# Five depthwise-convolution products of one channel tile on ScalarE and GpSimd, and a new plan

## The chip, the cores and the metric

The kernel runs on one core of a Trainium2 chip. The metric is the device time of one execution in microseconds (us), as the median of several runs. A core has TensorE (PE in the profile; its weight loads are PEld), VectorE (DVE), ScalarE (ACT), GpSimd (POOL) and SyncE (SP), which here only issues transfers. Each engine works through its own instruction list in order, and waits on semaphores for the others.

## What is computed

One layer of a decoder: 1024 prompt tokens and 8 sample tokens share all weights; the width is 1024.

```python
h = rmsnorm(x, g_mix);  u = h @ w_in                  # 1024 -> 512 pool, 512 value, 512 gate
glu = val * sigmoid(gate)                             # 512 channels
ya = pool_mixer(a)                                    # trailing means over 2/4/8/16 tokens, a linear map per group
yb = silu(layernorm(depthwise_conv31(glu) + b_dw))    # causal, 31 taps per channel
x = x + concat(ya, yb) @ w_out
x = x + cross_attn(rmsnorm(x, g_attn), mk, mv, w_q, w_o)   # 4 heads, 256 memory tokens
x = x + (silu(h @ w_gate) * (h @ w_up)) @ w_down      # h = rmsnorm(x, g_ffn)
y = rmsnorm(x, g_final)
```

Samples use cached keys and values and stored histories; the prompt's keys and values come from `mem_prompt` (`m @ w_k`, `m @ w_v`), and are outputs too, as are the new histories.

## The kernel before

Activations lie with channels on the 128 partitions and tokens along the free axis, even prompt tokens first (512), then odd (512), then the 8 samples. Every fp32 matmul is done as three passes over operands split in a high and a low part; the split is one copy (`split`, L466 to L479) that rounds, on ScalarE or GpSimd, and one subtraction, on VectorE or GpSimd. `split_by_dma` (L488 to L495) makes the low part with a negated copy and a transfer issued by GpSimd that adds the source.

The program is a list of tasks. Each task names the engines that may do it with a cost, the buffers that it reads and writes and a priority: its number in the list plus an entry of `NUDGE`. A planner, `Program.order` (L216), then walks through a timeline of its own costs and gives each task an engine and a place in that engine's order. `ORDER` is the list of pieces (letter and index) in which tasks are made, `CHOSEN` pins some tasks to one engine, `LEAD` says how many weight blocks ahead a block's loading and splitting are put, `SLACK` and `MARGINS` shape the planner's choice and its costs. Buffers come from tags with a few slots each: 3 scratch buffers (`scr`), 3 raw weights, 2 split weights, and in PSUM 2 of three banks (`mm`) and 2 of one bank (`ms`).

The stages, with their letters. Input projection: groups `g`, `v` (gate and value, four channel tiles) and `A` (pool channels), each a PE group in an `mm` buffer, which VectorE evicts (glu L829, a L935). Convolution of tile cg: with even and odd tokens apart, the 31 taps become two families. `C` (`conv_sums`, L749 to L769) makes 16 products of the sum of even and odd tokens with sums of neighbouring taps, on ScalarE or GpSimd into one of four slots of `cp`, which GpSimd or VectorE add to the odd half of `y`. `D` (`conv_parts`, L771) makes 31 products on VectorE, which fold into two PSUM accumulators `acc[0]` (16) and `acc[1]` (15), one instruction each, multiply and add (L781 for the first, L783 for the others; `cacc` in the profile). L791 to L802 then merge both with `y`. `s` does the sample tokens, `W` and `M` the pooling, `K` and `V` the memory's keys and values (kps, vps; evicted into the scratch buffers kf and vf and stored from there), `L` the layer norm.

`O` and `B` are the output projection, `q` the queries. Attention: scores `S` (L1126; maximum L1134, exponential L1143, normalising L1151), transposes `T` (L1165 to L1170), products `P` (`pv`, L1184 to L1189), and `a` to `e` for the samples, whose cached keys and values are multiplied on VectorE (spcache_k, spcache_v, L1223). `o`, then the pieces `u`, `x`, `y`, `z`, prepare the feed-forward part, which runs as a seven-product scheme (L1429), and the last stage (L1800 to L1857) ends with the final norm.

Of the kernel before, what the change touches and what calls it, by code (L numbers as in the profile page):

```python
# [1986 lines left out]
```

## Time and profile before

| | us |
|---|---|
| median of 3 runs | 1144.47 |
| lowest, highest | 1144.37, 1146.84 |
| the profiled execution | 1144.27 |
| its span, first to last instruction | 1142.5 |
| TensorE busy in it | 1120.8 |
| VectorE, ScalarE, GpSimd busy | 927.6, 499.7, 287.8 |

All rows that are shown come from the one profiled execution. A busy TensorE means that at least one matmul is under way; matmuls overlap, so it says nothing of their rate. In a table by stretch, the columns after each engine's busy time give its instruction count; the granted clock is the share of TensorE's full clock that it was allowed. A row of waits reads: engine and what it was about to do, then the instruction that ended the wait, the time in total, how often, and the longest. A row of a tile's instructions gives the shortest, the median and the longest duration in ns.

### The profile page before, as it was taken

What the parts mean: (1) busy time and instruction counts of PE and PEld (TensorE: products, weight loads), DVE (VectorE), ACT (ScalarE), POOL (GpSimd) and SP (SyncE); (2) the same over time, 40 slices, a digit from 0 to 9 for tenths busy, and PEclk for the clock granted to TensorE, in tenths of its full rate; (3) what the DMA queues carried; (4) which work ended last, traced back from release to release, by engine and by line L of the source; (5) the groups of instructions that cost most, each with busy time, mean ns of one, the idle gap of its engine ahead of it and who ended that gap; (6) DMA issues with size and microseconds to landing.
All of it is one profiled execution on the core that took longest, in us unless ns stands there. A gap on an engine that the chain in (4) does not pass through costs nothing.

```text
span 1142.5 us, 19533 instructions
## 1 busy us (share of the span) xinstructions
PE 1120.8 (98%) x7736; PEld 1067.4 (93%) x7736; DVE 927.6 (81%) x1514; ACT 499.7 (44%) x706; POOL 287.8 (25%) x327
## 2 busy tenths in 40 slices
PE   9999999999999989999999999999999999999996
PEld 8999988999999979999999999999999999999996
DVE  7999999776257886888888888988888798879744
ACT  7766648353243452445233333333433443332444
POOL 2689772133712201433000000000000123332011
PEclk9999999999999999999999999999999999999999
DMA  8444587433485687322424352254433697657612
GB/s 307 94 93 110 127 233 237 163 114 149 165 249 176 207 325 244 123 82 75 140 84 149 128 190 105 100 176 159 156 124 112 237 374 286 242 169 235 186 59 91
DMA packets 66252, 193.54 MB, mean 169 GB/s; under 512 B 8368, under 2 KB 12144, under 8 KB 64880
## 3 DMA queue, kind: packets, MB, share of 16 engines
q1 hardware_dynamic: 62128, 178.81, 43.8%
q0 software_dynamic: 3600, 13.13, 6.6%
q8 instruction: 61, 1.00, 0.4%
q10 hardware_dynamic: 432, 0.36, 0.1%
q14 instruction: 31, 0.25, 0.1%
HBM read 147.84 MB, written 44.43 MB: 168 GB/s over the span
## 4 chain that ended last, share of the span: by engine, by line
PE 78%; DVE 15%; DMA 4%; issue 1%; ACT 1%; POOL 0%; DVEq 0%; SPq 0%; ACTq 0%; POOLq 0%
PE pr L1429 49%; PE po L582 7%; DVE cacc L783 6%; PE ps L582 5%; PE fd L1800 4%; PE oa L582 4%; PE ob L582 4%; DVE spcache_k L1223 1%; PE vps L1027 1%; DMA spcache_k<-in_cache_k 1%; PE kps L949 1%; PE pv L1184 1%; DVE spcache_v L1223 1%; DVE xss L513 1%; DVE x L1854 1%
## 5 line engine op out<-in xcount | busy, mean ns | idle before, releaser
L1429 PEld LDWEIGHTS pr<-ab,wTb 128*128 128x128 f32 x1056 | 123.4, 190 | 2.3 <-issue 0.5
L1429 PE MATMUL pr<-ab,wTa 128*128 128x260 f32 x1056 | 124.9, 275 | 0.0
L1429 PE MATMUL pr<-ab,wTb 128*128 128x260 f32 x1056 | 124.3, 275 | 0.0
L1429 PEld LDWEIGHTS pr<-ab,wTa 128*128 128x128 f32 x1056 | 123.1, 190 | 1.3
L1429 PE MATMUL pr<-ab,wG 128*128 128x512 f32 x528 | 121.1, 380 | 0.0
L1429 PEld LDWEIGHTS pr<-ab,wG 128*128 128x128 f32 x528 | 96.9, 189 | 12.5 <-issue 0.5
L582 PE MATMUL ps<-xop,w 128*128 128x344 f32 x720 | 105.5, 309 | 0.0
L582 PEld LDWEIGHTS ps<-xop,w 128*128 128x128 f32 x720 | 105.0, 189 | 0.0
L1445 DVE TENSOR_TENSOR su<-pr,su 128x520 f32<-128x520 f32 (+1 forms) x112 | 77.3, 692 | 25.9 <-PE pr L1429 25.4
L1429 PEld LDWEIGHTS pr<-hb,dV 128*128 128x128 f32 x768 | 92.3, 190 | 2.2
L1429 PE MATMUL pr<-hb,dV 128*128 128x260 f32 x768 | 92.7, 275 | 0.0
L582 PE MATMUL ps<-xq,w 128*128 128x344 f32 x576 | 87.0, 310 | 0.0
L582 PE MATMUL po<-oo,w 128*128 128x344 f32 x576 | 84.7, 309 | 0.0
L582 PEld LDWEIGHTS po<-oo,w 128*128 128x128 f32 x576 | 84.3, 189 | 0.2
L582 PEld LDWEIGHTS ps<-xq,w 128*128 128x128 f32 x576 | 84.2, 189 | 0.1
L783 DVE SCALAR_TENSOR_TENSOR cacc<-glu,vec,cacc 128x502 f32<-128x502 f32 (+14 forms) x116 | 77.5, 739 | 0.1
L1429 PE MATMUL pr<-hb,dW 128*128 128x512 f32 x288 | 69.2, 379 | 0.0
L1456 POOL MEMSET su<- 128x16 f32 x22 | 2.4, 112 | 255.7 <-PE pr L1429 200.1
L1800 PE MATMUL fd<-ho,w 128*128 128x260 f32 (+1 forms) x432 | 64.3, 311 | 0.0
L1800 PEld LDWEIGHTS fd<-ho,w 128*128 128x128 f32 x432 | 59.8, 190 | 4.4 <-issue 0.5
L1445 DVE TENSOR_TENSOR x<-pr,x 128x512 f32<-128x512 f32 (+1 forms) x76 | 52.3, 690 | 12.7 <-PE pr L1429 11.6
L766 POOL TENSOR_TENSOR y<-y,cp 128x511 f32<-128x511 f32 (+14 forms) x46 | 57.6, 1254 | 14.9 <-DVE y L766 7.2
(314 smaller groups left out, 2164.7 us busy)
## 6 DMA issues: line engine op xcount, KB each, us to landing
gr<-in_w_gu SPq DMA_DIRECT2D x44, 512.0 KB, 3.4
hb<-su SPq DMA_DIRECT2D x16, 520.0 KB, 3.8
hb<-hb SPq DMA_DIRECT2D x16, 520.0 KB, 6.7
dr<-in_w_dn SPq DMA_DIRECT2D x16, 512.0 KB, 4.0
hb<-bh SPq DMA_DIRECT2D x14, 520.0 KB, 3.3
hb<-hb SPq DMA_DIRECT2D x14, 512.0 KB, 7.4
spcache_k<-in_cache_k SPq DMA_DIRECT2D x12, 512.0 KB, 5.2
ho<-hd SPq DMA_DIRECT2D x10, 520.0 KB, 6.3
```

The costliest lines, as they stand in the source:

```text
L513: add({"Pool": pool_tt(n), "DVE": dve(n)}, lambda e: e.tensor_tensor(total(), total(), sq[:, i, :n], ALU.add), [(sq, i), tkey], [tkey], lo ...
L582: e.matmul(placed(ps[:, c, :CW]), w[:, wi, cols], turns(x[:, xi, c * CW : (c + 1) * CW]), start=first and p == 0, stop=last and p == 2)
L766: add({"Pool": pool_tt(HALF), "DVE": dve(HALF)}, lambda e: e.tensor_tensor(yb[:, i, HALF + n : SEQ], yb[:, i, HALF + n : SEQ], cp[:, q, : ...
L783: e.scalar_tensor_tensor(acc[h][:, n:], src[:, : HALF - n], w, acc[h][:, n:], ALU.mult, ALU.add)
L949: e.matmul(placed(ps[:, 0, i * NMEM : (i + 1) * NMEM]), w[:, wi, block_cols(k)], turns(memg[k // 4][:, xi, k % 4]), start=(k == 0 and p == ...
L1027: e.matmul(placed(ps[:, m]), memg[k // 4][:, xi, k % 4, m * P : (m + 1) * P], turns(w[:, wi, col : col + 512]), start=(k == 0 and p == 0), ...
L1184: e.matmul(placed(ps[:, c]), v[:, vi, m, col : col + P], turns(pT[h][m][:, pi, sl]), start=(m == 0 and p == 0), stop=(m == 1 and p == 2))
L1223: e.scalar_tensor_tensor(piece[:, b], piece[:, b], 1.0, bc[:, b], ALU.mult, ALU.mult, accum_out=out(m)[:, first + b : first + b + 1])
L1429: e.matmul(placed(bank(c)), w[:, wi, cols(j)], turns(xs[0](j, xi)[:, c * n : (c + 1) * n]), start=onto is None and j == 0 and p == 0, stop ...
L1445: from_sums(sums, "DVE", dve, lambda e, src, sl: e.tensor_tensor(as_banks(o(sl), src), src, as_banks(a(sl), src), op), [akey], [okey])
L1800: e.matmul(placed(view(i)), w[:, wi, col : col + P], turns(hops[k][:, xi, half, lo - half * HALF + i * width // count : lo - half * HALF + ...
L1854: add({"DVE": dve(n * width)}, lambda e, i=i, n=n: e.tensor_tensor(x2[j][:, i : i + n, sl], x2[j][:, i : i + n, sl], fin[:, sl].unsqueeze( ...
```

## The change

- `conv_parts` for tile 3 (`OFFLOAD = (0, 0, 0, 5)`): the products n = 10 to 14 of the odd family no longer fold into `acc[1]` on VectorE. The first is written by ScalarE into a scratch buffer `part`; each of the other four is written by ScalarE or GpSimd into one of two halves of a second scratch buffer `ahead`, and added to `part` by GpSimd or VectorE. After the 26 products that stay, one addition on VectorE brings `part` into `acc[1]`.
- Normalising the probabilities may be done on ScalarE as well.
- `pv` may use single banks (`PV_MS`, empty), and for product 4 (`PV_FIRST`) both halves' matmuls are listed ahead of the copies.
- A new `ORDER`, `NUDGE` (about three times as many entries), `CHOSEN`, and new numbers in `LEAD`, `DOWN_BY_DMA`, `SLACK` and `MARGINS`.

```diff
 ORDER = (
-    "n0 g1 C0 v1 g2 s0 m6 v2 m1 g3 s1 m3 A1 A3 v3 m7 m4 m5 D0 A0 A2 m0 m2 K0 W3 C1 s3 K1 s2 K2 V1 W0 W1 C2 W2 M0 D1 Y0 M3 V0 "
+    "n0 g1 C0 v1 g2 s0 m5 v2 m1 g3 m7 m6 A1 A3 s1 v3 m3 m4 m0 D0 A0 A2 m2 K0 W3 C1 s3 K1 s2 K2 V1 W0 W1 D1 M3 C2 W2 M0 Y0 V0 "
...
-LEAD = {"w_k": 4, "w_v": 7, "w_out_a": 16, "w_q": 42, "w_in": 22, "w_out_b": 11, "w_o": 14}
+LEAD = {"w_k": 4, "w_v": 7, "w_out_a": 11, "w_q": 36, "w_in": 17, "w_out_b": 11, "w_o": 16}
...
-DOWN_BY_DMA = (0, 0, 0, 4)
+DOWN_BY_DMA = (0, 0, 0, 2)
...
+OFFLOAD = (0, 0, 0, 5)
+PV_MS = ()
+PV_FIRST = (4,)
...
-SLACK = {"Pool": 0.021, "ACT": 0.186, "DVE": 0.095, "PE": 0.044}
+SLACK = {"Pool": 0.076, "ACT": 0.109, "DVE": 0.057, "PE": 0.044}
...
+        aside = range(15 - OFFLOAD[cg], 15)
+        first = aside.start
+        part, ahead = [scr(f"{name}{cg}") for name in ("part", "ahead")] if aside else (None, None)
+
+        def aside_tap(n):
+            src, w = lambda: gb[:, i, HALF : HALF + HALF - n], vcol(V_CW, cg * CONV_K + 29 - 2 * n)
+            if n == first:
+                add({"ACT": act(HALF, ptrs=1)}, lambda e: e.activation(part[:, n:HALF], src(), AF.Copy, scale=w), [gk], [(part,)])
+                return
+            q = n % 2
+            at = slice(q * HALF, q * HALF + HALF - n)
+            add({"ACT": act(HALF, ptrs=1), "Pool": pool_ts(HALF)}, lambda e: (
+                e.activation(ahead[:, at], src(), AF.Copy, scale=w) if e is nc.scalar else
+                e.tensor_scalar(ahead[:, at], src(), w, 1.0, ALU.mult, ALU.mult)), [gk], [(ahead, q)])
+            add({"Pool": pool_tt(HALF), "DVE": dve(HALF)}, lambda e: e.tensor_tensor(
+                part[:, n:HALF], part[:, n:HALF], ahead[:, at], ALU.add), [(ahead, q), (part,)], [(part,)], lock=True)
+
+        for n in aside:
+            aside_tap(n)
+
         for n in range(16):
             for h in range(2):
-                if h + 2 * n < CONV_K:
+                if h + 2 * n < CONV_K and not (h and n in aside):
                     add({"DVE": 0.66 - 0.00105 * n}, lambda e, h=h, n=n: tap(e, h, n), [gk] + ([ak[h]] if n else []), [ak[h]])
+
+        if aside:
+            add({"DVE": dve(HALF)}, lambda e: e.tensor_tensor(
+                acc[1][:, first:], acc[1][:, first:], part[:, first:HALF], ALU.add), [ak[1], (part,)], [ak[1]])
...
-        add({"Pool": 0.95, "DVE": 0.53}, normalise, [(st, 2), (pr, i2)], [(pr, i2)], lock=True)
+        add({"Pool": 0.95, "DVE": 0.53, "ACT": 2 * act(NMEM, ptrs=1)}, normalise, [(st, 2), (pr, i2)], [(pr, i2)], lock=True)
...
+        for step, c in ((matmuls, 0), (matmuls, 1), (copies, 0), (copies, 1)) if n in PV_FIRST else ((matmuls, 0), (copies, 0), (matmuls, 1), (copies, 1)):
+            step(c)
```

More of the change, by code (lines that the diff above doesn't have):

```diff
@@ L60 @@
 PE_FIXED, PE_COLUMN = 0.0135, 0.000417
+OFFLOAD = (0, 0, 0, 5)
+PV_MS = ()
+PV_FIRST = (4,)
 SCORES_MM = (5, 12, 13, 15)
-SLACK = {"Pool": 0.021, "ACT": 0.186, "DVE": 0.095, "PE": 0.044}
+SLACK = {"Pool": 0.076, "ACT": 0.109, "DVE": 0.057, "PE": 0.044}
 MARGINS = {
     "early": {"PE": (0.93, 0.0), "DVE": (0.93, 0.0), "Pool": (1.01, 0), "ACT": (1.02, 0)},
-    "gated": {"Pool": (1.04, 0.04), "DVE": (1.01, 0.02), "PE": (0.95, 0.04), "ACT": (1.08, 0.06)},
+    "gated": {"Pool": (0.96, 0.04), "DVE": (1.01, 0.02), "PE": (0.95, 0.04), "ACT": (1.1, 0.04)},
     "down": {"DVE": (1.03, 0.103)},
-    "last": {"PE": (0.99, 0), "DVE": (1.02, 0.183)},
+    "last": {"PE": (1.08, 0), "DVE": (1.04, 0.243)},
 }
 NUDGE = {
[45 rows of a table removed]
[123 rows of a table added]
 }
@@ L120 @@
     "ACT": (
-        133, 179, 183, 207, 297, 502, 608, 660, 738, 907, 1374, 1406, 1578, 1617, 1647,
[5 rows of a table added]
     ),
     "DVE": (
-        26, 176, 404, 412, 477, 601, 609, 737, 745, 922, 1395, 1529, 2551, 2552, 2644, 2646,
[4 rows of a table added]
     ),
     "Pool": (
-        141, 184, 186, 198, 206, 388, 409, 415, 419, 520, 529, 539, 541, 555, 651, 654, 661, 664, 718, 719, 721, 725, 906, 1018, 1022,
-        1082, 1095, 1180, 1531, 1648, 2553,
[5 rows of a table added]
     ),
@@ L1150, in normalise @@
             for i in range(2):
-                e.tensor_scalar(pr[:, 2 * i2 + i], pr[:, 2 * i2 + i], st[:, 6 + i : 7 + i], 1.0, ALU.mult, ALU.mult)
-        add({"Pool": 0.95, "DVE": 0.53}, normalise, [(st, 2), (pr, i2)], [(pr, i2)], lock=True)
+                at, factor = pr[:, 2 * i2 + i], st[:, 6 + i : 7 + i]
+                if e is nc.scalar:
+                    e.activation(at, at, AF.Copy, scale=factor)
+                else:
+                    e.tensor_scalar(at, at, factor, 1.0, ALU.mult, ALU.mult)
+        add({"Pool": 0.95, "DVE": 0.53, "ACT": 2 * act(NMEM, ptrs=1)}, normalise, [(st, 2), (pr, i2)], [(pr, i2)], lock=True)
     def p_transpose(n):
@@ L1174, in pv, with matmuls, emit, copies @@
         h, dt = n // 2, n % 2
-        ps = mm_buf(f"pv{n}", 2)
+        apart = [ms_buf(f"pv{n}_{c}") for c in range(2)] if n in PV_MS else []
+        ps = None if apart else mm_buf(f"pv{n}", 2)
         col, v = (h % 2) * 256 + dt * P, vv[h // 2]
         oo = oop[n]
-        for c in range(2):
+        at = lambda c: apart[c] if apart else ps
+        bank = lambda c: apart[c][:] if apart else ps[:, c]
+        def matmuls(c):
             sl = slice(c * 512, (c + 1) * 512)
-            def emit(e, c=c, sl=sl):
+            def emit(e):
                 for m in range(2):
                     for p, (vi, pi) in enumerate(PASSES):
-                        e.matmul(placed(ps[:, c]), v[:, vi, m, col : col + P], turns(pT[h][m][:, pi, sl]),
+                        e.matmul(placed(bank(c)), v[:, vi, m, col : col + P], turns(pT[h][m][:, pi, sl]),
                                  start=(m == 0 and p == 0), stop=(m == 1 and p == 2))
-            add({"PE": pe(512, 6)}, emit, [(v, 0), (v, 1)] + [(pT[h][m], p, c) for p in range(2) for m in range(2)], [(ps,)])
-            add({"ACT": act(512, True)}, lambda e, c=c, sl=sl: e.activation(halves(oo[:, 0, sl]), drawn(ps[:, c]), AF.Copy), [(ps,)], [(oo, 0, c)])
-            add({"DVE": dve(512)}, lambda e, c=c, sl=sl: e.tensor_tensor(halves(oo[:, 1, sl]), drawn(ps[:, c]), halves(f32(oo[:, 0, sl])), ALU.subtract),
-                [(ps,), (oo, 0, c)], [(oo, 1, c)])
+            add({"PE": pe(512, 6)}, emit, [(v, 0), (v, 1)] + [(pT[h][m], p, c) for p in range(2) for m in range(2)], [(at(c),)])
+        def copies(c):
+            sl = slice(c * 512, (c + 1) * 512)
+            add({"ACT": act(512, True)}, lambda e: e.activation(halves(oo[:, 0, sl]), drawn(bank(c)), AF.Copy), [(at(c),)], [(oo, 0, c)])
+            add({"DVE": dve(512)}, lambda e: e.tensor_tensor(halves(oo[:, 1, sl]), drawn(bank(c)), halves(f32(oo[:, 0, sl])), ALU.subtract),
+                [(at(c),), (oo, 0, c)], [(oo, 1, c)])
+        for step, c in ((matmuls, 0), (matmuls, 1), (copies, 0), (copies, 1)) if n in PV_FIRST else ((matmuls, 0), (copies, 0), (matmuls, 1), (copies, 1)):
+            step(c)
     def s_query(h):
```

190 rows, old and new, of tables (CHOSEN, NUDGE, ORDER) are left out of this document.

## The prediction

> **What bounds the kernel now.** I read the page first: the span and the busy shares.
>
> ```profile
> span 1142.5 us, 19533 instructions
> PE 1120.8 (98%) x7736; PEld 1067.4 (93%) x7736; DVE 927.6 (81%) x1514; ACT 499.7 (44%) x706; POOL 287.8 (25%) x327
> ```
>
> The profiled execution took 1144.27 us, 1.77 us more than its span of 1142.5; the median of the three runs is 1144.47, so the sum below is made against 1144.3 and stands for the median to 0.2 us. TensorE (PE) is idle for 1142.5 − 1120.8 = 21.7 us in all. No edit changes a matmul, so only these idle microseconds can be won. The next view, the table by stretch, says where they lie (columns: stretch, its length, then busy us and instruction count of PE, weight load, VectorE (DVE), ScalarE (ACT) and GpSimd (POOL), granted clock, DMA share, GB/s).
>
> ```profile
> 20.00:140.00 120.00, 119.14 (x813) 117.89 (x814) 117.87 (x173) 81.89 (x113) 86.02 (x74) 1.00 0.45 113
> 140.00:152.00 12.00, 9.19 (x80) 8.84 (x79) 11.96 (x19) 5.42 (x6) 11.87 (x10) 1.00 0.88 216
> 152.00:163.00 11.00, 11.00 (x68) 10.01 (x67) 11.00 (x19) 6.49 (x8) 9.61 (x8) 0.84 0.85 241
> 163.00:187.00 24.00, 23.76 (x103) 18.74 (x101) 23.66 (x38) 16.53 (x19) 1.62 (x2) 1.00 0.65 202
> 187.00:205.00 18.00, 18.00 (x133) 17.63 (x132) 17.72 (x21) 11.60 (x15) 6.98 (x5) 1.00 0.98 323
> 340.00:360.00 20.00, 17.92 (x131) 17.38 (x130) 15.18 (x62) 7.36 (x18) 6.75 (x9) 1.00 0.73 236
> 380.00:425.00 45.00, 40.95 (x254) 35.26 (x252) 38.27 (x123) 23.30 (x52) 8.90 (x14) 1.00 0.81 276
> 425.00:1100.00 675.00, 675.00 (x4706) 640.81 (x4705) 562.99 (x817) 251.16 (x336) 89.92 (x123) 1.00 0.48 166
> 1100.00:1142.00 42.00, 33.38 (x283) 31.83 (x281) 21.98 (x42) 17.76 (x37) 7.98 (x10) 0.96 0.29 102
> ```
>
> Two places can be won by a schedule. One is the convolution: from 20 to 205 us VectorE is busy all the time (11.96 of 12, 11.00 of 11, 23.66 of 24), and PE loses 2.81 us at 140 to 152 and 0.24 at 163 to 187. The other is the attention, 2.08 us at 340 to 360 and 4.05 at 380 to 425. Together 9.2 us. The rest of the idle time is the start and the end, and from 425 to 1100 us there is none at all.
>
> The waits of PE and the timeline of VectorE show what the first place is.
>
> ```profile
> PE vps L1027 <- DVE kf L953: 1.9, 1, 1.9
> PE kps L949 <- DVE a L935: 0.9, 1, 0.9
> ```
>
> ```profile
> 144.28 6.63 DVE L783 SCALAR_TENSOR_TENSOR cacc<-glu,vec,cacc 128x510 f32<-128x510 f32 x10
> ...
> 150.82 0.68 DVE L953 TENSOR_TENSOR kf<-kps,side 128x512 f32<-128x512 f32 x1
> 151.42 2.69 DVE L783 SCALAR_TENSOR_TENSOR cacc<-glu,vec,cacc 128x505 f32<-128x505 f32 x4
> 154.02 0.68 DVE L953 TENSOR_TENSOR kf<-kps,side 128x512 f32<-128x512 f32 x1
> 154.62 7.84 DVE L783 SCALAR_TENSOR_TENSOR cacc<-glu,vec,cacc 128x503 f32<-128x503 f32 x12
> ```
>
> PE waits for evictions (a, kf) that stand on VectorE behind the last channel tile's products, the cacc rows. And the stall has a second price. The clock in two-microsecond stretches:
>
> ```profile
> 150.00:152.00 2.00, 0.35 (x2) 1.00 1.00 305
> 152.00:154.00 2.00, 2.00 (x7) 0.54 0.82 246
> 154.00:156.00 2.00, 2.00 (x8) 0.60 0.71 259
> 156.00:158.00 2.00, 2.00 (x19) 1.00 0.83 255
> ```
>
> Behind the 1.9 us wait the granted clock is 0.54 and 0.60 for 4 us: (0.46 + 0.40) × 2 = 1.7 us of matmul time lost. So this stall costs 2.81 + 1.7 = 4.5 us, not 2.8.
>
> **The change part by part.** (a) Five odd products of tile 3 (n = 10 to 14) leave VectorE. From the row of twelve, one takes 7.84 / 12 = 0.65 us of its queue, so 5 × 0.65 = 3.27 us. Back comes one addition from PSUM, priced by the eviction y<-cacc,y below (0.68). Net −2.6 us on VectorE, if the four additions of the side chain run on GpSimd.
>
> ```profile
> L763 ACT ACTIVATE cp<-y,csum x50: 695/706/722, 51.2 to 196.1; 128x509 f32<-128x509 f32 x4, 128x507 f32<-128x507 f32 x4, 128x506 f32<-128x506 f32 x4, 128x505 f32<-128x505 f32 x4
> L766 POOL TENSOR_TENSOR y<-y,cp x46: 1063/1266/1958, 52.0 to 198.2; 128x511 f32<-128x511 f32 x4, 128x510 f32<-128x510 f32 x4, 128x509 f32<-128x509 f32 x4, 128x508 f32<-128x508 f32 x4
> L766 DVE TENSOR_TENSOR y<-y,cp x14: 668/672/2055, 74.7 to 200.4; 128x500 f32<-128x500 f32 x3, 128x499 f32<-128x499 f32 x2, 128x497 f32<-128x497 f32 x2, 128x506 f32<-128x506 f32 x1
> L764 POOL TENSOR_SCALAR cp<-y,csum x6: 682/850/2657, 49.1 to 192.1; 128x511 f32<-128x511 f32 x2, 128x510 f32<-128x510 f32 x1, 128x508 f32<-128x508 f32 x1, 128x502 f32<-128x502 f32 x1
> ```
>
> ```profile
> L800 DVE TENSOR_TENSOR y<-cacc,y x4: 677/680/681, 77.6 to 199.1; 128x512 f32<-128x512 f32 x4
> ```
>
> The same shapes are already in the kernel: a product on ScalarE 0.71 us, on GpSimd 0.85; an addition on GpSimd 1.27, on VectorE 0.67. If all four additions went to VectorE the net would be −2.6 + 4 × 0.67 = +0.1. I take GpSimd, since it is busy for 1.62 of the 24 us from 163 to 187, and ScalarE (16.53 of 24) has room for 5 × 0.71 = 3.5 us: both covers are real. The merge is a new wait: it stands in VectorE's order and needs part, and behind it on VectorE are the splits of kT, the windows of the pooling and the evictions of vps, for which PE waits. If the cover were gone and the chain started only when VectorE is done, the merge would come 4 × 1.27 + 0.71 = 5.8 us later, 3.2 us more than was saved. What needs its result has time: y<-cacc,y of the last tile ran at 199.1 us, 37 us after the row of twelve ended.
>
> What of −2.6 reaches PE? With the order kept, almost nothing: the removed products are the last ones of the tile, at about 155 to 163 us, behind the stall, and PE loses only 0.24 us from 152 to 205. But VectorE is full for the whole stage, and the plan is written anew with 2.6 us less on it, so evictions can stand earlier. Bounds for this step: 3.2 us lost, and the whole 4.5 us won. A queue shortened by 2.6 us brings the 1.9 us wait to nothing and, with that, the slow clock: I take 1.9 of the 2.81 idle plus 1.4 of the 1.7, 3.3 us. I leave the 0.9 us wait for a, as the weights of w_k arrive barely in time there (DMA share 0.88).
>
> The Trainium skill (SBUF — State Buffer, "Who interferes with whom") speaks against moving additions to GpSimd: an instruction of VectorE with two SBUF inputs and one of GpSimd that reads SBUF lock each other out for a whole instruction. The rows agree that it happens (VectorE's y<-y,cp 2055 ns at most against a median of 672, so 1.38 us lost), and say that it is rare: the median lies 4 ns over the minimum. By the rule at its worst, four additions would cost VectorE 4 × 1.38 = 5.5 us and turn −2.6 into +2.9; by the median they cost nothing, which is what I take. At its worst the time would be 1144.3 + 2.9 − 2.4 (from b) = 1144.8, no change; I give that 0.03.
>
> (b) The attention stage: p·v product 4 issues both halves before its copies, normalising may run on ScalarE too, and scores, transposes, samples and weight loads (the LEAD numbers) get another order.
>
> ```profile
> PE pv L1184 <- DVE oo L1189: 2.5, 4, 1.5
> PE sc L1126 <- ACT probs L1143: 1.6, 1, 1.6
> PE pt L1165 <- DVE pT L1170: 0.9, 1, 0.9
> PE pv L1184 <- ACT probs L1143: 0.6, 1, 0.6
> PE ss L1236 <- DVE spcache_k L1223: 0.5, 1, 0.5
> L1151 DVE TENSOR_SCALAR probs<-probs,sm 128x256 f32<-128x256 f32 x14 | 4.3, 347 | 0.1
> L1143 ACT ACTIVATE probs<-sc,sm,r 128x256 f32<-128x256 f32 x26 | 14.4, 560 | 21.0 <-DVE sm L1136 13.5 <-DVE spcache_k L1223 7.4
> ```
>
> The five waits add up to 6.1 us. In pv, the two halves share one dependency key, so the second half waits for the copies of the first; putting both first takes one such wait of four away: 2.5 / 4 = 0.6 us. A normalising pair costs VectorE 2 × 0.35 us; on ScalarE, by its nearest row of that shape, 2 × 0.56. ScalarE is busy for 23.30 of 45 us at 380 to 425, VectorE 38.27, so a pair moved is 0.7 us off the fuller engine, behind which sc, pt and pv wait. Which of the moved pieces hit a wait the rows cannot say. Bounds: all 6.1 us won; or as much lost as the largest of these waits twice, 3.2. I take 40% of the 6.1, 2.4 us: the transfers of the sample caches (DMA share 0.81) stay and set some of the order.
>
> (c) The rest. Two down blocks of the last chunk get their low part by a subtraction of VectorE instead of a transfer that GpSimd issues, other splits change engine, the residual pieces x, u, y, z trade places, the costs of the last stage are rescaled, and the weights of w_in, w_q and w_out_a are asked for 5 to 6 blocks later on SyncE's queue (w_o 2 earlier).
>
> ```profile
> L477 DVE TENSOR_TENSOR hb<-hs,hb x12: 1215/1228/1772, 902.7 to 1027.5; 128x1040 fp32r<-128x1040 f32 x7, 128x1024 fp32r<-128x1024 f32 x5
> ```
>
> ```profile
> raw<-in_w_q SPq DMA_DIRECT2D x8, 512.0 KB, 3.2
> ```
>
> All this lies beside a PE with no idle time from 425 to 1100; VectorE has 675 − 563 = 112 us free there. Cost 0; with the cover gone, two subtractions of 1.2 us, and 3.2 us for each weight that is asked for only when PE wants it. The end (42 − 33.38 = 8.6 us idle) is a fixed chain of factors and stores; 0, and ±1 for the order.
>
> Sum: 1144.3 − 3.3 − 2.4 = 1138.6 us.
>
> **The rivals.** *The order does not reach the stalls.* The removed products lie behind the stall, the attention's waits are kept by PSUM buffers and cache transfers; PE then loses what it lost before: 1144.3 − 0.24 = 1144.1. For it: everything else from 425 on is covered. Against: VectorE, the engine named in three of the five waits, gets less to do in both stages.
>
> *The scratch buffers.* This one ends slower. part and ahead each hold one of the kernel's three scratch slots from the first side product to the merge, and kf, the eviction of a key group, needs a slot as well.
>
> ```profile
> L443 SPq DMA_DIRECT2D out_mem_k<-kf x4: 343/343/344, 151.5 to 193.8; - x4
> DMA to landing us min/median/max: 7.9/7.9/7.9
> ```
>
> A kf holds its slot until its transfer has landed, 151.5 + 7.9 = 159.4 us; the second one is written at 154.02. With one slot left, it waits 5.4 us, and PE behind it, for its two PSUM buffers are then full. If the attention's 2.4 come all the same, 1144.3 + 5.4 − 2.4 = 1147.3; and a wait of that length takes the clock down as above, 1.7 more, 1149.0. It decides if the pair is taken before the second kf is written (154 us) and held over it; it does nothing if the chain is put at 163 to 187, where GpSimd is free.
>
> The clock is a rival on a smaller scale, inside the forecast: it may stay low for the 4 us though the wait is gone, and then step (a) gives 1.9 and the time is 1144.3 − 1.9 − 2.4 = 1140.0. I give it 0.1 of the forecast's chance. The Trainium skill (TensorE: Matmul & The Clock Gate, "Part 1: The HAM clock gate") has the clock fall to half after an idle window of about 3.4 us. The trace disagrees in the length, since 1.9 us of idle time were enough here while 1.6 us at 356 us left it at 1.00; by the rule a wait of 1.9 us costs its length alone, which gives the same 1140.0.
>
> **How the numbers follow.** Forecast 0.64; order does not reach 0.15; additions that lock VectorE out 0.03; scratch buffers 0.18. What a measurement of this kernel can tell from no change is 0.2%, 2.3 us: below 1142.2 is faster, above 1146.8 slower. So faster 0.64, same 0.15 + 0.03 = 0.18, slower 0.18. The forecast's own range is its bounds: all idle time of both stages and the slow clock won is 1144.3 − 9.2 − 1.7 = 1133.4, with 1 us at the end 1132.4; the range reaches over the second rival to the third at 1149.0: 1132.5 to 1149.0.
>
> **What would show it.** Right: PE's wait for kf gone from 140 to 165 us and the clock 1.00 there; 26 odd and even products of tile 3 on VectorE and the side additions on GpSimd; PE's waits for oo under 2 us in all; PE idle from 140 to 425 about 4.5 us instead of 9.2. Wrong: a clock of half anywhere new, waits of kf or vf on part, or idle time of PE between 425 and 1100 us, which would mean that one of the covers of (c) was thinner than I read it.

## The result: 1.0% slower

The changed kernel takes 1156.22 us (median of 4 runs, 1154.2 to 1159.31) against 1144.42 us on the same chip: a ratio of 1.0103, 95% interval 1.0083 to 1.0123. That is 11.8 us slower, where 5.8 us faster was forecast, and above the forecast's range, which ended at 1149.0. The profiled execution took 1159.31 us, 15.0 more than that of before, and the comparison below is of these two. It is the slowest of the four (two took 1154.2), so some of what it shows, the wait at 1007 us perhaps, is not in every execution. First the page's span and busy times, after:

```profile
span 1157.4 us, 19546 instructions
PE 1123.1 (97%) x7736; PEld 1069.9 (92%) x7736; DVE 937.5 (81%) x1529; ACT 500.7 (43%) x709; POOL 276.2 (24%) x314
```

The span grew by 14.9 us. PE is busy 2.3 us longer with the same 7736 matmuls, so more of them ran at a lower clock; the other 12.6 us are idle time. The table by stretch says where (columns as in the prediction), before:

```profile
135.00:240.00 105.00, 101.95 (x643) 93.59 (x642) 94.91 (x134) 64.78 (x76) 44.54 (x32) 0.98 0.67 200
345.00:430.00 85.00, 78.87 (x531) 72.30 (x529) 67.98 (x237) 39.29 (x95) 16.87 (x27) 1.00 0.69 232
990.00:1030.00 40.00, 40.00 (x288) 37.92 (x287) 33.06 (x48) 14.02 (x19) 15.05 (x20) 1.00 0.67 231
1100.00:1142.50 42.50, 33.38 (x283) 31.83 (x281) 21.98 (x42) 17.76 (x37) 7.98 (x10) 0.95 0.28 100
```

and after:

```profile
135.00:240.00 105.00, 98.90 (x622) 90.64 (x621) 96.17 (x135) 63.81 (x77) 36.99 (x29) 0.98 0.67 201
345.00:430.00 85.00, 76.68 (x522) 70.89 (x521) 67.71 (x232) 43.41 (x103) 15.39 (x23) 1.00 0.69 229
990.00:1030.00 40.00, 36.64 (x274) 34.95 (x273) 30.10 (x46) 11.84 (x15) 11.72 (x15) 1.00 0.61 198
1100.00:1157.40 57.40, 44.31 (x323) 41.42 (x321) 29.20 (x54) 18.89 (x36) 9.46 (x10) 0.90 0.21 75
```

PE's idle time, stretch minus busy, went from 3.05 to 6.10 us in the convolution, from 6.13 to 8.32 in the attention, from 0 to 3.36 in the down stage (where there had been none from 425 on), and from 9.12 to 13.09 in the last stage, where the granted clock fell as well: 12.6 us in all. PE's waits after, the longest first:

```profile
PE pr L1558 <- DVE x L1574: 3.4, 1, 3.4
PE fd L1929 <- DVE x L1938: 3.2, 1, 3.2
PE kps L1064 <- DVE kf L1068: 2.9, 1, 2.9
PE fin_ps L1961 <- DVE fin L604: 1.7, 1, 1.7
PE ss L1365 <- DVE spcache_k L1352: 1.6, 1, 1.6
...
PE pmap L1085 <- ACT vf L1147: 1.4, 1, 1.4
PE kps L1064 <- ACT w L557: 1.4, 1, 1.4
...
PE pv L1307 <- DVE oo L1315: 0.9, 3, 0.4
```

**The convolution.** The wait for kf did not go, it grew from 1.9 to 2.9 us. VectorE's timeline shows why: eight products still stand between the first and the second eviction.

```profile
148.79 0.68 DVE L1068 TENSOR_TENSOR kf<-kps,side 128x512 f32<-128x512 f32 x1
149.39 5.31 DVE L874 SCALAR_TENSOR_TENSOR cacc<-glu,vec,cacc 128x507 f32<-128x507 f32 x8
154.61 0.68 DVE L1068 TENSOR_TENSOR kf<-kps,side 128x512 f32<-128x512 f32 x1
```

And the offload took nothing off VectorE, for the side chain's four additions and the merge are all there:

```profile
L890 DVE TENSOR_TENSOR part<-part,ahead x4: 665/668/680, 194.5 to 200.3; 128x501 f32<-128x501 f32 x1, 128x500 f32<-128x500 f32 x1, 128x499 f32<-128x499 f32 x1, 128x498 f32<-128x498 f32 x1
...
L902 DVE TENSOR_TENSOR cacc<-cacc,part x1: 678/678/678, 201.4 to 201.4; 128x502 f32<-128x502 f32 x1
```

4 x 0.668 + 0.678 = 3.35 us came for the 3.27 of the five products. The queue up to the last window of the pooling (which pmap needs) is shorter by the five products, but the new plan filled the gap with work that GpSimd or a later place had. VectorE's groups from 140 us to that window, before (to 185.2) and after (to 187.7; columns: count, busy us, mean ns, idle time before it):

```profile
L783 DVE SCALAR_TENSOR_TENSOR cacc<-glu,vec,cacc 128x511 f32<-128x511 f32 (+14 forms) x29 | 19.4, 741 | 0.0
...
L910 DVE TENSOR_TENSOR win<-win 128x1022 f32<-128x1022 f32 (+1 forms) x3 | 3.6, 1210 | 0.0
L477 DVE TENSOR_TENSOR opa<-yf,opa 128x1032 fp32r<-128x1032 f32 x2 | 2.4, 1224 | 0.0
```

```profile
L874 DVE SCALAR_TENSOR_TENSOR cacc<-glu,vec,cacc 128x511 f32<-128x511 f32 (+14 forms) x24 | 16.3, 740 | 0.1
...
L1025 DVE TENSOR_TENSOR win<-win 128x1022 f32<-128x1022 f32 (+1 forms) x4 | 4.8, 1212 | 0.0
L568 DVE TENSOR_TENSOR opa<-yf,opa 128x1032 fp32r<-128x1032 f32 x3 | 3.7, 1224 | 0.0
L1029 DVE TENSOR_TENSOR win<-a 128x512 f32<-128x512 f32 x3 | 3.5, 1162 | 0.0
L568 DVE TENSOR_TENSOR kT<-kf,kT 128x512 fp32r<-128x512 f32 x2 | 2.1, 1058 | 0.0
...
L857 DVE TENSOR_TENSOR y<-y,cp 128x506 f32<-128x506 f32 (+1 forms) x2 | 1.4, 678 | 0.0
```

Minus 3.1, then plus 1.2, 1.3 and, from the last row, 1.4 (before, no y<-y,cp addition of VectorE lay in that stretch). The two rows in between are old work that took longer: one win<-a addition, at 139.0 us, 2.12 us where it had been 0.68, and one kT<-kf subtraction 1.43 us where the mean had been 0.70. GpSimd was adding or subtracting beside each of the two. Together they cost 2.2 us, two thirds of what the five products had given.

**The down stage.** A subtraction for the weights of a later unit (dt<-dr) stands in VectorE's queue ahead of an eviction that is ready. Its transfer was issued at 999.32 us and took 10.8 us; VectorE stood for 5.4 us until it landed.

```profile
1004.12 0.70 DVE L1574 TENSOR_TENSOR x<-pr,x 128x520 f32<-128x520 f32 x1 [0.64 <-PE pr L1558]
1010.20 0.43 DVE L1760 TENSOR_TENSOR dt<-dr 128x256 f32<-128x256 f32 x1 [5.38 <-DMA dr<-in_w_dn]
1010.54 0.68 DVE L1574 TENSOR_TENSOR x<-pr,x 128x512 f32<-128x512 f32 x1
```

**The last stage.** VectorE's eviction x waits for a store, and PE for the eviction; the clock follows. The row of VectorE's wait before, when PE did not wait for x, and after:

```profile
DVE x L1809 <- DMA out_yT<-x: 4.6, 3, 2.1
```

```profile
DVE x L1938 <- DMA out_yT<-x: 6.7, 2, 4.6
```

```profile
1126.00:1128.00 2.00, 0.00 (x0) 0.00 (x0) 0.00 (x0) 0.00 (x0) 0.00 (x0) 1.00 0.07 24
1128.00:1130.00 2.00, 1.02 (x5) 1.02 (x6) 1.22 (x4) 1.04 (x3) 0.52 (x2) 0.81 0.00 0
1130.00:1132.00 2.00, 2.00 (x12) 2.00 (x11) 1.33 (x3) 0.62 (x2) 0.66 (x1) 0.50 0.00 0
1132.00:1134.00 2.00, 2.00 (x17) 2.00 (x17) 0.00 (x0) 0.00 (x0) 0.00 (x0) 0.84 0.00 0
```

Behind the wait of 3.2 us the clock costs (0.19 + 0.50 + 0.16) x 2 = 1.7 us.

### The profile page after: what moved, and what is told of

Read it like the earlier page. It is cut to its first block, busy times and chain, and to the rows that moved or that the text cites. A ratio compares the mean times of both kernels' runs of the same rounds, so it can differ in the third digit from the quotient of the medians.

```text
span 1157.4 us, 19546 instructions
## 1 busy us (share of the span) xinstructions
PE 1123.1 (97%) x7736; PEld 1069.9 (92%) x7736; DVE 937.5 (81%) x1529; ACT 500.7 (43%) x709; POOL 276.2 (24%) x314
## 4 chain that ended last, share of the span: by engine, by line
PE 72%; DVE 18%; DMA 6%; ACT 2%; issue 2%; POOL 0%; DVEq 0%; ACTq 0%; SPq 0%; POOLq 0%
PE pr L1558 47%; PE po L673 7%; DVE cacc L874 6%; PE ps L673 5%; PE fd L1929 5%; PE ob L673 4%; PE oa L673 3%; DMA spcache_k<-in_cache_k 2%; DVE spcache_k L1352 1%; DMA dr<-in_w_dn 1%; PE pv L1307 1%; DVE x L1983 1%; DVE spcache_v L1352 1%; DVE y L857 1%; DVE w L568 1%
## 5 line engine op out<-in xcount | busy, mean ns | idle before, releaser
L1558 PEld LDWEIGHTS pr<-ab,wG 128*128 128x128 f32 x528 | 97.1, 189 | 12.6 <-issue 0.5
L874 DVE SCALAR_TENSOR_TENSOR cacc<-glu,vec,cacc 128x503 f32<-128x503 f32 (+14 forms) x111 | 74.5, 738 | 0.2
L1929 PE MATMUL fd<-ho,w 128*128 128x260 f32 (+1 forms) x432 | 66.7, 317 | 3.2 <-DVE x L1938 3.2
L1558 PE MATMUL pr<-ab,wU 128*128 128x512 f32 x264 | 60.4, 379 | 0.0
```

The source lines that it names most:

```text
L874: e.scalar_tensor_tensor(acc[h][:, n:], src[:, : HALF - n], w, acc[h][:, n:], ALU.mult, ALU.add)
L1558: e.matmul(placed(bank(c)), w[:, wi, cols(j)], turns(xs[0](j, xi)[:, c * n : (c + 1) * n]), start=onto is None and j == 0 and p == 0, stop ...
L1929: e.matmul(placed(view(i)), w[:, wi, col : col + P], turns(hops[k][:, xi, half, lo - half * HALF + i * width // count : lo - half * HALF + ...
```

## The experiments

The expectations speak of PE's lost time: summed over the matmul rows of a stretch, the time from one start to the next beyond what the columns need at the full clock (213 ns for a pass of 512, whose rows stand 215 to 216 ns apart in undisturbed stretches). It holds idle time, slow clock and small gaps; the gaps hardly differ between the kernels. For the convolution the column behind it gives the idle time and the loss by the slow clock alone. One profiled execution each; the ratio is to the kernel before on the same chip. On the four chips used, the kernel before had medians of 1144.0 to 1145.7 us, so kernels from different chips are compared by the ratio (0.1% is 1.1 us) and not by the median.

| kernel | median, us | ratio (95%) | conv. 135-240 | idle + slow clock | attention 345-430 | down 990-1030 | from 1100 |
|---|---|---|---|---|---|---|---|
| before | 1144.4 | 1 | 8.2 | 3.0 + 1.7 | 11.0 | 0.9 | 2.4 |
| changed | 1156.2 | 1.0103 (1.0083-1.0123) | 11.4 | 6.1 + 1.7 | 12.8 | 4.5 | 8.4 |
| u1_no_offload | 1158.2 | 1.0116 (1.0097-1.0135) | 12.5 | 7.1 + 1.7 | 10.5 | 0.9 | 9.6 |
| u7_gpsimd | 1162.9 | 1.0154 (1.0132-1.0175) | 15.7 | 9.9 + 1.7 | 12.0 | 4.1 | 8.4 |
| u3_one_row | 1153.8 | 1.0077 (1.0056-1.0098) | 12.6 | 6.1 + 3.0 | 12.1 | 5.8 | 1.9 |
| u2_unit_late | 1158.6 | 1.0127 (1.0107-1.0147) | 12.5 | 7.1 + 1.7 | 10.7 | 3.7 | 8.3 |
| u10_rows_unit | 1150.6 | 1.0038 (1.0023-1.0052) | 11.5 | 6.2 + 1.7 | 13.3 | 3.6 | 1.9 |
| u4_kf_early | 1156.5 | 1.0106 (1.0078-1.0133) | 11.5 | 5.8 + 1.7 | 9.9 | 6.2 | 8.5 |
| u6_mended | 1150.7 | 1.0043 (1.0024-1.0062) | 10.0 | 5.4 + 0 | 12.4 | 2.1 | 1.9 |
| u9_mended_first | 1149.5 | 1.0026 (1.0013-1.0039) | 9.1 | 5.1 + 0 | 12.0 | 3.3 | 1.8 |
| u8_half_cache | 1157.3 | 1.0101 (1.0076-1.0125) | 11.4 | 6.4 + 1.4 | 9.1 | 5.8 | 8.2 |
| b3_five_gone | 1146.7 | 1.0008 (0.9993-1.0023) | 8.2 | 3.0 + 1.7 | 12.2 | 0.9 | 2.3 |
| b4_mended | 1148.7 | 1.0031 (1.0019-1.0043) | 8.4 | 4.4 + 0 | 15.9 | 1.1 | 1.9 |
| b5_gone_early | 1145.6 | 0.9996 (0.9980-1.0012) | 7.5 | 3.4 + 0 | 9.1 | 0.9 | 2.2 |
| b6_first_act | 1143.1 | 0.9986 (0.9975-0.9997) | 7.0 | 3.2 + 0 | 10.4 | 0.9 | 2.3 |
| b7_first_kf | 1144.4 | 0.9991 (0.9979-1.0002) | 5.9 | 2.6 + 0 | 11.6 | 0.9 | 1.7 |
| b8_first_rows | 1144.8 | 0.9988 (0.9975-1.0000) | 6.1 | 2.5 + 0 | 12.3 | 0.9 | 1.8 |

Names with u start from the changed kernel, with b from the one before. Order edits put given tasks right behind another in the issued list, with everything else in its place (`MOVES`: tasks, then the one they go behind; in the changed kernel 763 to 788 are the products left of tile 3, 401, 470 and 498 the first three kf evictions).

**The offload undone, the plan kept.**

```diff
-                add({"ACT": act(HALF, ptrs=1)}, lambda e: e.activation(part[:, n:HALF], src(), AF.Copy, scale=w), [gk], [(part,)])
+                add({"ACT": act(HALF, ptrs=1)}, lambda e: None, [gk], [(part,)])
...
-            add({"Pool": pool_tt(HALF), "DVE": dve(HALF)}, lambda e: e.tensor_tensor(
-                part[:, n:HALF], part[:, n:HALF], ahead[:, at], ALU.add), [(ahead, q), (part,)], [(part,)], lock=True)
+            add({"Pool": pool_tt(HALF), "DVE": dve(HALF)}, lambda e: tap(e, 1, n), [(ahead, q), (part,)], [(part,)], lock=True)
```

> The changed kernel with its five products taken back: nothing runs on ScalarE and GpSimd for them, and in the five places of VectorE's queue where the four additions and the merge stood (about 194 to 201 us) stand the five products themselves (0.65 us each against 0.67), in the same order of everything else. Theory (the 12 us come from the new plan, the offload itself costs and brings nothing): no change against the changed kernel, 1156.2 within 1 us. Rival (the offload costs the time, through its additions, its products on ScalarE and GpSimd or their locks): the time comes back toward 1144.4, by at least 3 us.

1158.2 us, against 1156.2: the time does not come back. The offload itself is worth nothing here, and the loss is the plan's. (PE's wait at 1007 us is missing in this profile. The late transfer, issued at 997.75 us, had landed by 1004.8, and VectorE stood for it 1.6 us instead of 5.4.)

**The additions on GpSimd,** as the prediction had assumed them.

```diff
-            add({"Pool": pool_tt(HALF), "DVE": dve(HALF)}, lambda e: e.tensor_tensor(
+            add({"Pool": pool_tt(HALF), "DVE": dve(HALF)}, lambda e: nc.gpsimd.tensor_tensor(
                 part[:, n:HALF], part[:, n:HALF], ahead[:, at], ALU.add)
```

> The changed kernel with the four additions of the side chain on GpSimd instead of VectorE, in the same places of the order. Theory (nothing of PE hangs on them at 190 to 205 us): 1156.2 within 1 us, VectorE's busy time down by 4 x 0.67 = 2.7, GpSimd's up by 4 x 1.27 = 5.1. Rival 1 (the 2.7 us freed on VectorE reach PE): 1153.5. Rival 2 (the additions lock VectorE out, 1.38 us each, or the merge comes 3.2 us late): up to 5.5 us later, 1161.7.

Slower than the changed kernel by 0.5%, 5.8 us (1.0154 against 1.0103): rival 2. The other additions of the same queue, y<-y,cp on VectorE, in the changed kernel and here (130 to 206 us; min/median/max ns), and what GpSimd needs for one of its own here:

```profile
L857 DVE TENSOR_TENSOR y<-y,cp x9: 662/674/1076, 169.5 to 200.9; 128x506 f32<-128x506 f32 x1, 128x505 f32<-128x505 f32 x1, 128x504 f32<-128x504 f32 x1, 128x503 f32<-128x503 f32 x1
```

```profile
L857 DVE TENSOR_TENSOR y<-y,cp x9: 673/948/2026, 169.6 to 200.0; 128x506 f32<-128x506 f32 x1, 128x505 f32<-128x505 f32 x1, 128x504 f32<-128x504 f32 x1, 128x503 f32<-128x503 f32 x1
...
L890 POOL TENSOR_TENSOR part<-part,ahead x4: 1392/1512/1570, 196.2 to 201.6; 128x501 f32<-128x501 f32 x1, 128x500 f32<-128x500 f32 x1, 128x499 f32<-128x499 f32 x1, 128x498 f32<-128x498 f32 x1
```

VectorE gave 2.7 us of additions away, and these nine took 2.8 us longer in sum (6.45 to 9.30); the chain ended 1.5 us later (merge at 202.98 against 201.45), and ysum came later still, lengthened to 2.91 us beside a split on GpSimd. PE then waited 1.9 us for it, and 1.3 us for weights of w_out_a, whose transfer GpSimd issued 1.9 us later, behind the first two additions. That an instruction of VectorE with two SBUF inputs contends with one of GpSimd that reads SBUF is what the Trainium skill says (SBUF — State Buffer, "Who interferes with whom"), and here the trace agrees: median 948 ns for 674 while GpSimd adds beside it. The two profiled executions differ by 3.7 us, and the convolution's lost time by 4.3; what the medians have beyond that is not traced.

**Single-row stores.** The store of two rows of x covers a span of columns in each; the even row's next eviction, to other columns, waits for it. The program's own keys, `(x2[j], i, c)`, are set for each span c, so the planner's timeline did not have this wait.

```diff
-            dma(lambda i=i, n=n: io["yT"][2 * j + i : 2 * j + i + n][:, :, sl].rearrange("n p t -> p n t"), lambda i=i, n=n: x2[j][:, i : i + n, sl],
-                4 * P * width * n, r=keys[i : i + n])
+            def stores(e, i=i, n=n):
+                for row in range(i, i + n):
+                    e.dma_start(io["yT"][2 * j + row][:, sl], x2[j][:, row, sl])
+
+            add({"SP": 0.05}, stores, keys[i : i + n], (), nbytes=4 * P * width * n)
```

> The changed kernel with each store of two rows of the result given as two stores of one row; nothing else. Theory (the even row's next eviction waits for the store of both rows of the span before, though it writes other columns): the waits x <- out_yT (6.7 us in all) go, with them PE's fd wait of 3.2 and most of the half clock behind it (1.7), so 1156.2 - 4.9 = 1151.3, within 1.5 us; bounds 3.2 and 6.5 less. Rival (the last stage is longer since its factors are ordered otherwise, and the store is not to blame): 1156.2, or later by up to 1 us, for the added stores.

The last stage's lost time falls by 6.5 us, to what it was before; the row of the last stage, to be held against 1100.00:1157.40 above:

```profile
1100.00:1153.90 53.90, 44.33 (x333) 41.52 (x331) 30.48 (x55) 19.83 (x38) 9.02 (x10) 0.95 0.23 80
```

13.09 us of idle time became 9.57, and the waits for fd, for fin and of x for the store are gone. The time fell by less, from 1.0103 to 1.0077 (3.0 us). In the profiled execution two other stages lost more, the down stage 1.3 us (5.8) and the convolution 1.2, and in both the slow clock took more than in the changed kernel's profile.

**The down unit.** First one subtraction, then the whole group of its subtractions, behind the evictions that they block.

```diff
+MOVES = [((2921,), 2880)]
```

> The changed kernel with one step of VectorE's queue moved: the first subtraction for the weights of the next down unit, which at 1005 to 1010 us waits 5.4 us for its transfer, goes behind the eviction x<-pr that stood behind it. Theory (a late transfer at the head of the queue blocks an eviction that is ready): PE's wait of 3.4 us at 1007 goes, time 1156.2 - 3.4 = 1152.8, within 1 us. Rival (PE would wait for that weight itself a little later, the 3.4 us only move): 1156.2.

The 3.4 us became waits of 0.9 and 1.3 us for the next evictions: the second subtraction of the pair still stood ahead of one, and a split that waited 1.1 us for ScalarE ahead of the other. The time did not fall (1158.6), as the rival had it, though not by its mechanism: PE did not wait for the weight itself. The whole group, with the single-row stores:

```diff
+MOVES = [((2921, 2922, 2923, 2924, 2925), 2888), ((2926,), 2909), ((2892, 2890), 2926)]
```

> The changed kernel with two edits alone: single-row stores and the early down unit's subtractions behind three evictions. Theory: 6.4 from the last stage and 2.4 from the down stage (what these two gave in the kernel with all four mended), 1156.2 - 8.8 = 1147.4, within 2 us, the convolution's lost time as in the changed kernel (11.4). Rival (part of the four edits' gain was the convolution's): 1150 to 1152.

A ratio of 1.0038 for 1.0103: about 7.4 of the expected 8.8 us come back, within the theory's 2 us, though the two intervals leave 4.6 to 10.2. (The median of 1150.6 comes from a chip on which the kernel before takes 1145.5.) The stores gave theirs (8.4 to 1.9 lost from 1100 on); the wait of 3.4 us is gone, but three waits for x, 1.8 us together, took its place, so the moved subtractions pay about half of theirs.

**kf earlier.**

```diff
+MOVES = [((775, 770, 777, 772, 779, 774), 470), ((782, 786, 787, 788), 498)]
```

> The changed kernel with ten of the last tile's products moved in VectorE's queue: six of the eight ahead of the second kf eviction go behind it, four of those ahead of the third go behind that. Theory (PE stands for 2.9 us because kf is queued behind products, and loses another 1.7 us to the half clock that follows): 1156.2 - 4.6 = 1151.6, within 1.5 us, the clock 1.00 from 152 to 163. Rival (PE then waits for the next weights, which GpSimd is splitting and the transfers bring at a share of 0.88): the wait only changes its name, 1156.2 to 1154.5.

The rival, and its name was too narrow. PE's waits from 135 to 240 us:

```profile
PE pmap L1087 <- DVE win L1040: 1.9, 1, 1.9
PE kps L1066 <- DVE a L1052: 1.2, 1, 1.2
PE vps L1144 <- POOL w L570: 1.1, 1, 1.1
PE vps L1144 <- DVE w L570: 0.8, 1, 0.8
```

The 2.9 us for kf are gone and the clock is 1.00 from 152 to 165, but VectorE's last window ends only 1.4 us earlier (186.3 for 187.7), so that PE, which gets there sooner, waits 1.9 us for it, and the clock falls at 187 instead. Lost time 11.5 against 11.4.

**The same questions in the old order.** Five products left out (`b3`), kf earlier (`b4`, with both halves of two p.v products ahead of their copies and the stores), and products left out and kf earlier (`b5`).

```diff
-                    add({"DVE": 0.66 - 0.00105 * n}, lambda e, h=h, n=n: tap(e, h, n), [gk] + ([ak[h]] if n else []), [ak[h]])
+                    gone = cg == 3 and h and n in range(10, 15)
+                    add({"DVE": 0.66 - 0.00105 * n}, (lambda e: None) if gone else lambda e, h=h, n=n: tap(e, h, n), [gk] + ([ak[h]] if n else []), [ak[h]])
```

> The kernel before with the five products (odd taps n = 10 to 14 of the last channel tile) left out altogether and nothing put in their place, the order kept: the output lacks those five terms. It bounds what an offload of just these products can bring in the old order: VectorE is 3.27 us shorter from 155 to 163 us. Theory (they stand behind the stall for kf, and PE waits for little after it): 1144.4, at most 0.5 us less; the kf wait of 1.9 and the slow clock stay. Rival (VectorE is the bound of the whole stage, so that each microsecond off its queue reaches PE): 1141.1.

As the theory had it, 1.0008: not even a free removal of these five products shortens the old order, and the 1.9 us for kf stay.

```diff
+MOVES = [((756, 757, 758, 759, 760, 761), 401), ((762, 763, 764, 765), 470), ((774, 775, 776, 777), 498), ((1343,), 1340), ((1385,), 1382)]
```

> The kernel before, without the offload, with four order edits: kf evictions ahead of six, four and four of the last tile's products; both halves of two p.v products ahead of their copies; single-row stores. Theory (the wait for kf and its half clock can be had by order alone, 3.5 us; the second half of the p.v product waits only for the copies of the first, 1.5 us; the stores hold nothing up here, 0): 1144.4 - 5.0 = 1139.4, within 1.5 us. Rival (as in the changed kernel with kf early, PE then waits for weights that GpSimd and VectorE split): the 3.5 us come back as other waits by 190 us, 1142.9.

Slower by 0.3%: both parts of the theory fell. In the convolution the wait changed its name (lost time 8.4 for 8.2):

```profile
PE pmap L972 <- DVE win L925: 3.2, 2, 1.7
```

The wait and its half clock did go, but 1.4 us more of idle time came for the 1.7 of clock. In the attention the oo waits fell from 2.5 to 0.8 us, but ss waited 2.6 for spcache_k and pt 2.4 for prow, and behind each of these two waits the clock fell: of the 4.9 us more that were lost, 3.3 are slow clock.

> The kernel before with two things at once: the five products left out (the output lacks those terms) and the kf evictions ahead of six, four and four products as in the order edit that alone only moved PE's wait from kf to the last windows. Theory (VectorE is the bound from 140 to 205 us, so a shorter queue and an order that lets PE use it are both needed): no wait for kf, the waits for win (3.2 us in all with the order edit alone) nearly gone, PE's lost time from 135 to 240 us 5.0 instead of 8.2 to 8.4. Rival (the waits in this stage are set by weights and transfers): 8 us or more, as with each edit alone.

In between: 7.5 lost, not 5.0. The waits for kf are gone and the one for win is down to 0.4, as a shorter queue together with the order should do, but PE then waits 2.1 us for the transfers of w_v. The idle time is no less than before (3.4 us for 3.0); what is gained is the slow clock. So with VectorE's queue shorter the weights limit this stage at once.

**First products on ScalarE.** The product that starts each sum is a plain scaling; ScalarE can write it to the same PSUM bank, with no buffer and no addition. For tiles 2 and 3:

```diff
-                e.tensor_scalar(acc[h][:], src, w, None, ALU.mult)
+                if cg > 1:
+                    nc.scalar.activation(acc[h][:], src, AF.Copy, scale=w)
+                else:
+                    e.tensor_scalar(acc[h][:], src, w, None, ALU.mult)
```

> The kernel before with another offload in its own order: the first product of each half of channel tiles 2 and 3 (a plain scaling, 0.75 us on VectorE) runs on ScalarE (about 0.7 us), four in all; it needs no buffer and no addition. Theory (work taken from VectorE ahead of kf reaches PE): VectorE is 3 us earlier by 145 us, the kf wait of 1.9 us and the half clock behind it go: 1144.4 - 3 = 1141.4, within 1 us. Rival 1 (PE's wait for a and the weights come up behind it): 1143.5. Rival 2 (ScalarE's queue stands there, and VectorE waits for the first product): up to 3 us slower, 1147.4.

Faster than both kernels, by little: 0.9986 (0.9975 to 0.9997). VectorE reaches kf 3 us earlier (before, 150.82):

```profile
147.86 0.69 DVE L956 TENSOR_TENSOR kf<-kps,side 128x512 f32<-128x512 f32 x1
```

```profile
PE pmap L973 <- ACT vf L1035: 1.4, 1, 1.4
PE oa L582 <- DMA w<-in_w_out_a: 1.0, 1, 1.0
PE vps L1030 <- DVE kf L956: 0.4, 1, 0.4
PE kps L952 <- DVE kf L956: 0.4, 1, 0.4
```

VectorE keeps its lead, and its last window ends at 182.4 us instead of 185.2. Yet PE's idle time in this stage stays (3.2 us for 3.0): the wait of 1.9 us is cut into two of 0.4, and waits for vf and for weights take up what that frees. The half clock is gone, and in these two profiles that is the whole gain of the stage.

> As the last, with the two kf evictions also four and two products earlier and single-row stores in the last stage. Theory: kf's wait gone for certain, 0.4 us less in the last stage, so 1144.4 - 3.9 = 1140.5, within 1.2 us. Rival (the moved products make the windows late, as before): 1143 to 1145.

> The kernel before with the first products of channel tiles 2 and 3 on ScalarE and single-row stores, nothing else. Theory: the 1.6 us of the first and 0.4 us of the stores add up, 1144.9 - 2 = 1142.9 where the runs of before lie at 1144.9, a ratio of 0.9982. Rival (the stores cost as much in issues as they save): as with the first products alone, 0.9986.

Both lose about 6 us in the convolution, 2 less than before (1.7 by the clock, 0.5 of idle time), but their times (0.9991 and 0.9988) are not to be told apart from `b6`. In the old order the stores bring 0.5 us of lost time and nothing in the total.

**Mended versions of the changed kernel.** `u6`: stores, kf earlier, one opa subtraction (753) behind the last window (601), the down unit's group. `u9`: the same without kf, with the first products on ScalarE.

```diff
+MOVES = [((775, 770, 777, 772, 779, 774), 470), ((782, 786, 787, 788), 498), ((753,), 601), ((2921, 2922, 2923, 2924, 2925), 2888), ((2926,), 2909), ((2892, 2890), 2926)]
```

> The changed kernel with the offload kept and four places of its order mended: single-row stores, kf evictions ahead of the products, one opa subtraction (1.22 us) behind the last window instead of ahead of it, and the whole group of subtractions for the early down unit moved behind three evictions. Theory (the loss is a sum of separate order faults of the new plan: 6.4 us in the last stage, 3.5 to 6 in the down stage at 1007, 3 to 4 in the convolution): 1156.2 - 6.4 - 3.5 - 2.5 = 1143.8, within 2.5 us. Rival (VectorE is simply too full from 140 to 190 us, and the faults only move): no better than 1148.

> The changed kernel with single-row stores, the early down unit's subtractions behind three evictions, the opa subtraction behind the last window, and the first product of each half of channel tiles 2 and 3 on ScalarE (3 us off VectorE); the kf evictions stay where the plan has them. Theory (in the convolution PE's lost time follows VectorE's sum of work): lost time from 135 to 240 us 11.4 - 3 = 8.4 or less, and the whole 1156.2 - 6.4 - 2.4 - 3 = 1144.4, within 2 us. Rival (the waits there are the plan's order and weights): 11 us stay lost, 1147.5 or more.

Ratios of 1.0043 and 1.0026: 6.9 and 8.8 us of the 11.8 come back, not 12, and neither is clear of `u10`, which has the stores and the down unit alone (1.0038). So the times do not show that the edits in the convolution pay. In the profile of `u9` the convolution has 1.0 us less of idle time than the changed kernel and no half clock; the edit of the first products and that of the opa subtraction were not told apart. Of the 3.0 us that `u9` still loses, its profile has 2.4 in the down stage and 0.9 in the convolution.

**Half the sample caches.**

```diff
-                dma(lambda piece=piece: piece[:], lambda m=m, first=first: io[cache][2 * h + m][:, first : first + count],
+                half = count // 2
+                dma(lambda piece=piece, half=half: piece[:, :half], lambda m=m, first=first, half=half: io[cache][2 * h + m][:, first : first + half],
...
-                            e.scalar_tensor_tensor(piece[:, b], piece[:, b], 1.0, bc[:, b], ALU.mult, ALU.mult,
+                            e.scalar_tensor_tensor(piece[:, b], piece[:, b % (count // 2)], 1.0, bc[:, b], ALU.mult, ALU.mult,
```

> The changed kernel with only half of the samples' key and value caches transferred; VectorE still does all its products, on the half that is there twice (so the samples' attention is not that of the reference). Theory (in the attention the caches' transfers set PE's waits, whatever the order of p.v, since VectorE waits 7.1 us there for them): PE's lost time from 345 to 430 us falls from 10 to 13 us to 8 or less, the time by 3 us or more. Rival (the order of VectorE's and PE's work sets them): the lost time stays at 10 to 13.

Between the two: 9.1 lost, below all nine profiles with that attention (9.9 to 13.3; but `b5`, in the old order, has 9.1 as well) and above the 8 named; PE's wait for spcache_k is gone. That the transfers make a part of the attention's waits fits this, but one profile does not show it, and the time has nothing of it (1.0101).

## Why the prediction was wrong

*(a) Minus 3.3 us in the convolution; measured plus 3.2.* Three steps failed. "If the four additions run on GpSimd": the plan put them on VectorE, and the net was the +0.1 that I had worked out and set aside; on GpSimd they would have been worse (`u7`), by the rival "additions lock VectorE out", to which I gave 0.03 because the stretched additions were rare in the old profile. That said how seldom the two met in that plan, and not what a meeting costs in another; in the new plan two of them cost VectorE 2.2 us even with the four additions on VectorE. "A queue shortened by 2.6 us brings the 1.9 us wait to nothing": the five products stood behind kf (`b3` leaves them out and keeps the wait), and the new plan left eight others between two evictions. And beneath both, that a wait removed is time won: in a stage where VectorE is busy all the time, `u4` and `b4` removed the kf wait and lost as much at the next window. Even 3 us off VectorE's queue ahead of the wait (`b6`) left PE's idle time as it was; in the old order no edit took more than 0.5 us off it. The 1.7 us of slow clock behind such a wait were sized well: it fell again, at 156 or 187. Why the new plan idles PE 3.1 us longer in this stage stays open in part: undoing the offload (`u1`) or moving kf (`u4`) does not bring it back, and the best of the mended orders (`u9`) still has 5.1 us for 3.0.

*(b) Minus 2.4 us in the attention; measured plus 1.8 in the profile.* The term for p.v was more than right: three waits for oo, 0.9 us, instead of four with 2.5. The 40% were not; other waits took their place (ss 1.6 us for spcache_k and 1.2 for pT, pt 1.5 for pT, sc 1.1 for oo), as in `b4`, where the same kind of edit went with 4.9 us more of lost time, 3.3 of them slow clock. Nine profiles with the new order average 11.7 us lost (9.9 to 13.3), six with the old one 11.1 (9.1 to 12.3): no gain, and no loss that I could tell from the scatter.

*(c) The rest at 0, the end at 0 within 1 us; measured plus 3.6 and plus 6.0.* This is the largest of the three, and the only one that experiments give back: the single-row stores and the down unit's order bring the ratio from 1.0103 to 1.0038, about 7 of the 11.8 us. It is not the whole of the miss: with both mended the kernel is still 0.4% slower than before, where 0.5% faster was forecast. I read 112 us of free time on VectorE as a cover, but a queue in order has none for the instruction behind one that waits for a transfer: 3.4 us, near the 3.2 I had named for a late weight, though not PE waited for the weight but an eviction behind it. In the last stage I looked at the order of factors and not at what an eviction waits for; the row "x <- out_yT" stood in the old profile as well (4.6 us in 3 waits), without a wait of PE for x behind it. `u3` shows it: 6.5 us, half clock included.

The scratch rival did not occur: part was written at 185.5 us and merged at 201.4, when no kf waited. The wait came on the other side: GpSimd's product into ahead stood 28.0 us, until VectorE had split vf; with these products gone (`u1`) the time stayed, so no cost of it shows. "Order does not reach the stalls" was nearest in mechanism, and missed that a new order makes stalls of its own. The forecast's signs of being wrong (a new half clock, idle time of PE between 425 and 1100) both showed. Two slips changed nothing: the idle time named as a sign of being right should be 9.2 - 1.9 - 2.4 = 4.9 us and not 4.5, and the lower bound comes out as 1132.4 and not 1132.5.

## What to carry to other kernels

Where an engine is full through a whole stage, don't price an edit by the wait that it removes: in `u4`, `b4`, `b5` and `b6` TensorE waited about as long in all, or longer, for the next thing that it needed (a window, vf, weights). Ask what that next need is, and when it is ready. Where a plan is written anew, the risk lies in the stages the change doesn't name; look there for instructions fed by a late transfer that stand ahead of an eviction, for evictions that wait for a store of other columns, and for additions on GpSimd beside a full VectorE.
